# Weight tiles of 16 KiB per partition in place of 8 KiB, and the residual added behind the third expert's gate

## The chip, the cores and the metric

The kernel runs on one core of a Trainium2 chip. The metric is the device time of one execution in microseconds (us). One KiB is 1024 bytes, one MiB 1024 KiB; GB/s are powers of ten.

## The reference

One layer of an encoder over 256 positions of width 2048, in float32. A mixer (attention with forget gates beside a state-space scan, between one input and one output projection) is followed by a mixture of 16 experts, of which each position uses two, and a gated embedding of the layer's own input `p`:

```
h   = layer_norm(ALPHA * h + hybrid_mixer(h), ln1_g, ln1_b)
moe = sum over e of combine[:, e] * ((silu(h @ w_gate[e]) * (h @ w_up[e])) @ w_down[e])
ple = sigmoid(h @ w_ple_gate) * (p @ w_ple)
out = layer_norm(ALPHA * h + moe + ple, ln2_g, ln2_b)
```

`w_gate` and `w_up` are 16 x 2048 x 1024, `w_down` is 16 x 1024 x 2048: 8 MiB each per expert, 384 MiB in all. `w_ple_gate` is 2048 x 2048 (16 MiB).

## The kernel before

**Two halves.** `front` computes the mixer; TensorE is its limit. `back` does the first layer norm, the transposed activations `hT`, the router, the 16 experts, the gated embedding and the last norm. All large weights come through one stream of loads.

**The ring.** `plan_loads` writes a list of loads, in the order in which `back` will use them: `p`, one quarter of column 0 of `w_ple_gate`, and for each expert eight pairs of a gate and an up tile, then eight down tiles. Ahead of the gate of experts 3, 6, 9 and 12 (`PLE_AT`) stand the pieces of one column of 512 of `w_ple_gate` and the piece of `w_ple`. A tile is 128 partitions by 8 KiB, 1 MiB. `Ring` hands out slots: `fill` gives each free slot the next load of the list, and `take` gives the slot of the tile that is about to be used back to the list of free slots. 16 slots go round (pools `ring0` to `ring3`, 4 each), and the pool `bonus` has two that are used once and whose place then becomes the accumulator `acc`. The loads are issued in order on SyncE's queue (SP). A load into a slot waits until TensorE has read the slot's last tile, and with it wait all loads behind it.

**An expert.** `gather` picks the rows of two experts at a time with one-hot matmuls (64 places for each expert; L681). For each expert `gate_up` (L711) makes the two sums `pgu`, `hidden` (L718 to L725) the activated product and its transpose, `down` (L758) the output in the bank `py`, and `give_back` (L735, L739) adds it to `acc` by one-hot matmuls and VectorE. While VectorE and ScalarE work in `hidden`, and between the parts of `give_back`, TensorE's program has matmuls of the next expert's gate. `ple_gate` (L803, L817) comes behind `down` of experts 3, 6, 9 and 12 in the code, and its matmuls L803 are laid between those of the next gate or of the same expert's.

**What stands around the edit.** The first quarter of column 0 (`PLE_FIRST`) is multiplied in the router phase, between the router's matmuls and the first `gather`. `residual` forms ALPHA times the first norm's output: `row_bank` (L882) copies rows of gain and bias to all partitions with matmuls into the bank `py`, which has one buffer, and VectorE multiplies and adds from it into `acc` (L897, L898), in four rounds for four columns of 512. It is issued behind the gate of expert 0. At expert 7 (`OV_AT`) a conditional block for positions that found no place (`overflow`) makes the engines meet.

Of the kernel before, what the change touches and what calls it, by code (L numbers as in the profile page):

```python
# [7 lines left out]
F32 = mybir.dt.float32  # L8
# [16 lines left out]
RING0, RING1, RING2, RING3 = 4, 4, 4, 4  # L25
PLE_AT = (3, 6, 9, 12)
PLE_FIRST = 1
OV_AT = 7

# [9 lines left out]
class Ring:  # L39


    def __init__(self, pool, bufs):
        self.loads, self.n, self.pools, self.spare, self.tiles = [], 0, [], [], {}
        self.once = None
        self.add(pool, bufs)
        self.spare = []
# [26 lines left out]
def plan_loads(nc, ring, i):  # L73

    def rows(src, row0, nrow, col0, ncol):
        return lambda t: nc.sync.dma_start(
            t[:, :nrow // 128 * ncol].rearrange("p (k f) -> p k f", f=ncol),
            src[row0:row0 + nrow, col0:col0 + ncol].rearrange("(k p) f -> p k f", p=128))

    def pairs(src, b):  # L80

        return lambda t: nc.sync.dma_start(t, src[b * 256:(b + 1) * 256, :].rearrange("(p r) f -> p (r f)", r=2))

    def pair_cols(src, g, col0):
        def load(t):
            for b in range(2):
                nc.sync.dma_start(
                    t[:, b * 1024:(b + 1) * 1024].rearrange("p (r f) -> p r f", r=2),
                    src[g * 512 + b * 256:g * 512 + (b + 1) * 256, col0:col0 + 512].rearrange("(p r) f -> p r f", r=2))
        return load  # L90

    def quarter(src, fb0, q):
        def load(t):
            for dh in range(2):
                nc.sync.dma_start(
                    t.rearrange("p (k d f) -> p k d f", d=2, f=256)[:, :, dh, :],
                    src[fb0 * 128:(fb0 + 4) * 128, dh * 1024 + q * 256:dh * 1024 + (q + 1) * 256]
                    .rearrange("(k p) f -> p k f", p=128))
        return load

    L = ring.loads
    L.append(("p", rows(i["p"][0, 0], 0, 256, 0, 256)))
    def ple_gate(c, parts):
        return [(("pg", c, g), pair_cols(i["w_ple_gate"][0], g, c * 512)) for g in parts]

    L += ple_gate(0, range(PLE_FIRST))
    for e in range(NE):
        if e in PLE_AT:
            c = PLE_AT.index(e)
            L += ple_gate(c, range(0 if c else PLE_FIRST, 4))  # L110
            L.append((("ple", c), rows(i["w_ple"][0], 0, 256, c * 512, 512)))
        for k in range(8):
            L.append((("g", e, k), pairs(i["w_gate"][0, e], k)))
            L.append((("u", e, k), pairs(i["w_up"][0, e], k)))
        if e < NE - 1:
            L += [(("d", e, k), rows(i["w_down"][0, e], k * 128, 128, 0, DM)) for k in range(8)]
        else:
            L += [(("d", e, k), quarter(i["w_down"][0, e], 4 * (k % 2), k // 2)) for k in range(8)]


def front(ctx, tc, i, dbg=lambda *a: None):
    nc = tc.nc
    const = ctx.enter_context(tc.tile_pool(name="const", bufs=1))
    ring = Ring(ctx.enter_context(tc.tile_pool(name="ring0", bufs=1)), RING0)
# [36 lines left out]
    for j, n in enumerate(("ln1_g", "ln1_b")):  # L161
        nc.gpsimd.dma_start(lnT[:, j, :].rearrange("p (b r) -> p b r", r=2),
                            i[n][0].rearrange("(b p r) -> p b r", p=128, r=2))
# [3 lines left out]
    for r in range(2):  # L167
        nc.gpsimd.dma_start(fr.wr.rearrange("p (b r) e -> p r b e", r=2)[:, r, :, :NE],
                            i["w_router"].rearrange("(b p r) e -> p r b e", p=128, r=2)[:, r])
# [19 lines left out]
    def load_w(src, row0, nrow, col0, ncol, behind=False):  # L189
        t = ring.tile(0)  # L190
# [287 lines left out]
    ring.add(fr.es_bonus.enter_context(tc.tile_pool(name="bonus", bufs=1, side="right")), 2)  # L478
# [49 lines left out]
    es_mix.close()  # L528
    es_ps.close()
# [3 lines left out]
def back(ctx, tc, i, out, fr, dbg=lambda *a: None):  # L533
# [5 lines left out]
    ring.spare += [0] * RING0  # L539
# [46 lines left out]
    for k2 in range(8):  # L586
        ps = banks[k2].rearrange("p (k t) -> p k t", k=2)
        for r in range(2):
            k = 2 * k2 + r
            for t in range(NT):  # L590
                nc.tensor.transpose(ps[:, r, t * 128:(t + 1) * 128], h[:, t, k2 * 256 + r:(k2 + 1) * 256:2], ident)
# [19 lines left out]
    for t in range(NT):  # L611
        router_mm = nc.tensor.matmul(pr[:, t, :], r4[:, t * 128:(t + 1) * 128], sel4, start=True, stop=True)
# [54 lines left out]
    def gather(e):  # L667
# [7 lines left out]
        for k4 in range(4):  # L675
            ps = mt_psum([128, 4, 2, CAP])
            ks = range(4 * k4, 4 * k4 + 4)
            for k in ks:
                cols = slice(k // 2 * 256 + k % 2, (k // 2 + 1) * 256, 2)
                for t in range(NT):  # L680
                    nc.tensor.matmul(ps[:, k % 4], h[:, t, cols], oh[:, t, :, 0, :], start=t == 0, stop=t == 1)  # L681
# [21 lines left out]
    def gate_up(e, xg):  # L703
        pgu = [psum.tile([128, 512], F32, name="pgu", tag="gu", bufs=2) for _ in range(2)]
        for k2 in range(8):
            for j in range(2):
                w = v2(ring.take(("gu"[j], e, k2)), FE)
                for r in range(2):
                    k = 2 * k2 + r
# [6 lines left out]
    def hidden(pgu):  # L716
# [5 lines left out]
        for j in range(4):  # L722
            nc.tensor.transpose(ps[:, j, :], hid[:, j * 128:(j + 1) * 128], ident)  # L723
# [4 lines left out]
    def give_back(e, cm, y, cols, n, pss):  # L728


        for t in range(NT):
# [5 lines left out]
            for dh, hs in H2:  # L737
                a = acc[:, t, dh * 1024 + cols:dh * 1024 + cols + n]
                nc.vector.scalar_tensor_tensor(a, ps[dh], cw[:, t, e:e + 1], a, op0=OP.mult, op1=OP.add)  # L739
# [11 lines left out]
    def down(e, hidT, cm):  # L751
        py = psum.tile([128, 2, 512], F32, name="py", tag="y", bufs=1)
        for fb in range(8):
            w = ring.take(("d", e, fb))
            fh, j = divmod(fb, 4)
            for c in range(2):
                for dh, hs in H2:
                    nc.tensor.matmul(py[hs, c, :], hidT[:, j, fh * 64:(fh + 1) * 64],  # L758
                                     w[:, dh * 1024 + c * 512:dh * 1024 + (c + 1) * 512],
                                     start=fb == 0, stop=fb == 7)  # L760
            ring.fill()
# [11 lines left out]
    def down_last(e, hidT, cm):  # L773
        py = psum.tile([128, 2, 512], F32, name="py", tag="y", bufs=1)
        y = y_parts()
        for q in range(4):
            pq = py[:, q // 2, (q % 2) * 256:(q % 2) * 256 + 256]
            for f2 in range(2):
                w = ring.take(("d", e, 2 * q + f2)).rearrange("p (k d f) -> p k d f", d=2, f=256)
                for j in range(4):  # L780
                    for dh, hs in H2:
                        nc.tensor.matmul(pq[hs], hidT[:, j, f2 * 64:(f2 + 1) * 64], w[:, j, dh, :],  # L782
                                         start=f2 + j == 0, stop=f2 + j == 4)
                ring.fill()
# [9 lines left out]
    pgs = {}  # L794

    def ple_sums(c, parts):
        pg = pgs[c] = pgs.get(c) or [pl_psum() for _ in range(NT)]
        for g in parts:
            w = v2(ring.take(("pg", c, g)), 512)
            for r in range(4):  # L800
                k = 4 * g + r
                for t in range(NT):
                    nc.tensor.matmul(pg[t], hT[:, k, t * 128:(t + 1) * 128], w[:, r, :],  # L803
                                     start=k == 0, stop=k == KB - 1)
            ring.fill()

    def ple_gate(c):
        cs = slice(c * 512, (c + 1) * 512)
        ple_sums(c, range(0 if c else PLE_FIRST, 4))
        pg = pgs.pop(c)  # L810
        w = v2(ring.take(("ple", c))[:, :1024], 512)
# [10 lines left out]
    def overflow():  # L822
# [9 lines left out]
        with tc.If(n_over > 0):  # L832
            with tc.For_i(0, NE, 1) as e:
# [6 lines left out]
                for fh in range(2):  # L840
                    pgs = [psum.tile([128, 512], F32, name="pgu", tag="gu", bufs=2) for _ in range(NT)]
                    pus = [pl_psum() for _ in range(NT)]
                    for k in range(KB):
                        for j, (src, pz) in enumerate(((i["w_gate"], pgs), (i["w_up"], pus))):
                            w = wload(ow[j], src, e, k // 2 * 256 + k % 2, fh * 512, 2)
# [24 lines left out]

    with tc.issue_after(router_mm.ins):
        ple_sums(0, range(PLE_FIRST))
# [14 lines left out]
    def residual():  # L887

        fr.es_bonus.close()
        accp = ctx.enter_context(tc.tile_pool(name="accp", bufs=1, side="right"))  # L890
        acc = accp.tile([128, NT, DM], F32, name="acc")
        for c in range(4):
# [6 lines left out]
        return acc  # L899

    for e in range(NE):
# [3 lines left out]
        if e == 0:  # L905
            with tc.issue_after(gated.ins):
                acc = residual()
# [79 lines left out]
```

## Time and profile before

| what | value |
|---|---|
| median of three runs | 1470.08 us (1469.17 to 1472.7) |
| the profiled execution | 1471.18 us, its span 1469.5 us |
| TensorE busy (PE) | 1397.5 us, 95% |
| VectorE, ScalarE, GpSimd busy | 459.3, 296.9, 63.0 us |
| moved by DMA | 499.95 MB, mean 340 GB/s |

The expert part runs from about 448 us to 1450 us of the span; what comes before is the mixer, the first norm and the router. On the page the span is cut into 40 slices, so each figure there stands for 36.7 us. PE is TensorE's matmul side, PEld its weight load, DVE VectorE, ACT ScalarE, POOL GpSimd, SP SyncE. A matmul of the source in fp32 is two instructions in the trace. `pgu`, `py`, `mt`, `pl` are PSUM tiles, `ring` a weight tile.

### The profile page before, as it was taken

The page shows a single profiled execution, that of the slowest core. Times are in us where ns is not written, and L with a number is a line of the kernel's source. Part 1 is how long each engine was busy: PE and PEld are TensorE (multiplying, and loading weights), DVE is VectorE, ACT ScalarE, POOL GpSimd, SP SyncE. Part 2 cuts the span into 40 slices and gives each one's busy share as a digit, 9 for nine tenths or more (in the row PEclk, how much of TensorE's full clock was granted, in tenths as well). Part 3 has the DMA queues.
Part 4 walks back from the last instruction along what each step waited for, and adds up shares of the span by engine and source line. Part 5 has one row for each costly group of instructions (what it writes and reads, how often), then busy time and mean ns, then how long its engine had stood idle before and what let it go on. Part 6 is the DMA issues. An engine that isn't in the chain of part 4 may idle for free. (4 is left out here: it accounts for less than half of the span.)

```text
span 1469.5 us, 15853 instructions
## 1 busy us (share of the span) xinstructions
PE 1397.5 (95%) x6531; PEld 722.8 (49%) x6531; DVE 459.3 (31%) x777; ACT 296.9 (20%) x477; POOL 63.0 (4%) x80
## 2 busy tenths in 40 slices
PE   7999999999989999999999999799999999999993
PEld 5877888787884443334324323433343342344332
DVE  4486784646552331202022002112020220202116
ACT  4465554444340010001001000100010010011000
POOL 3000101201000000000000000000000000000002
PEclk9999999999999999999999999999999999999997
DMA  8645456457955799999999999999999999999994
GB/s 268 202 163 182 158 175 227 158 182 278 349 229 231 310 410 420 411 420 419 420 420 409 419 420 420 365 421 408 421 390 420 420 407 420 420 420 419 420 394 160
DMA packets 116720, 499.95 MB, mean 340 GB/s; under 512 B 12692, under 2 KB 25436, under 8 KB 68260
## 3 DMA queue, kind: packets, MB, share of 16 engines
q1 hardware_dynamic: 115200, 495.42, 85.3%
q0 software_dynamic: 1408, 3.43, 0.9%
q8 instruction: 53, 0.87, 0.2%
q14 instruction: 23, 0.19, 0.0%
q10 hardware_dynamic: 36, 0.05, 0.0%
HBM read 496.70 MB, written 2.16 MB: 339 GB/s over the span
## 5 line engine op out<-in xcount | busy, mean ns | idle before, releaser
L711 PE MATMUL pgu<-ring,xg 128*64 128x512 f32 x2048 | 476.8, 598 | 4.4 <-DMA ring<-in_w_gate 2.6
L711 PEld LDWEIGHTS pgu<-ring,xg 128*64 128x64 f32 x2048 | 138.9, 136 | 294.9 <-issue 277.9
L758 PE MATMUL py<-ring,hidT 128*64 128x512 f32 x960 | 209.3, 594 | 4.8 <-ACT hidT L725 4.8
L205 DVE TENSOR_TENSOR wl<-ring,wh 128x1024 fp32r<-128x1024 f32 x128 | 156.3, 1224 | 139.0 <-ACT wh L204 133.8
L204 ACT ACTIVATE wh<-ring 128x1024 fp32r<-128x1024 f32 x128 | 135.4, 1059 | 171.2 <-PE pj L211 151.9
L719 DVE TENSOR_TENSOR hid<-hid,pgu 128x512 f32<-128x512 f32 x16 | 11.0, 687 | 465.6 <-ACT hid L718 465.6
L209 PE MATMUL pj<-wh,xh 128*128 128x512 f32 x384 | 154.2, 403 | 1.1 <-ACT xh L186 1.0
L210 PE MATMUL pj<-wl,xh 128*128 128x512 f32 x384 | 154.0, 402 | 0.0
L211 PE MATMUL pj<-wh,xl 128*128 128x512 f32 x384 | 153.3, 401 | 0.0
L758 PEld LDWEIGHTS py<-ring,hidT 128*64 128x64 f32 x960 | 67.7, 137 | 136.4 <-issue 127.3
L803 PE MATMUL pl<-ring,hT 128*128 128x512 f32 x256 | 127.8, 619 | 0.0
L749 DVE TENSOR_TENSOR y<-py,y 128x512 fp32r<-128x512 f32 (+1 forms) x34 | 22.4, 660 | 256.2 <-ACT y L748 256.2
L718 ACT ACTIVATE hid<-pgu 128x512 f32<-128x512 f32 x16 | 9.6, 597 | 431.9 <-PE pgu L711 431.9
L209 PEld LDWEIGHTS pj<-wh,xh 128*128 128x128 f32 x384 | 72.9, 190 | 18.3 <-ACT xh L186 2.2
L211 PEld LDWEIGHTS pj<-wh,xl 128*128 128x128 f32 x384 | 72.8, 190 | 16.5 <-DVE xl L187 0.2
L210 PEld LDWEIGHTS pj<-wl,xh 128*128 128x128 f32 x384 | 72.8, 190 | 16.2
L803 PEld LDWEIGHTS pl<-ring,hT 128*128 128x128 f32 x256 | 43.0, 189 | 73.0 <-issue 71.2
L748 ACT ACTIVATE y<-py 128x512 fp32r<-128x512 f32 (+1 forms) x34 | 19.5, 572 | 253.6 <-PE py L758 207.5
L681 PE MATMUL mt<-oh,h 128*128 128x128 f32 x512 | 63.8, 287 | 6.3 <-PEq L832 6.3
L681 PEld LDWEIGHTS mt<-oh,h 128*128 128x128 f32 x512 | 63.1, 202 | 7.1 <-issue 7.0
L209 PE MATMUL pj<-wh,moh 128*128 128x512 f32 (+1 forms) x160 | 56.7, 354 | 0.0
L210 PE MATMUL pj<-wl,moh 128*128 128x512 f32 (+1 forms) x160 | 56.5, 353 | 0.0
(259 smaller groups left out, 975.2 us busy)
## 6 DMA issues: line engine op xcount, KB each, us to landing
ring<-in_w_gate SPq DMA_DIRECT2D x128, 1024.0 KB, 18.9
ring<-in_w_up SPq DMA_DIRECT2D x128, 1024.0 KB, 19.0
ring<-in_w_down SPq DMA_DIRECT2D x120, 1024.0 KB, 19.9
ring<-in_w_in SPq DMA_DIRECT2D x48, 1024.0 KB, 5.1
ring<-in_w_out SPq DMA_DIRECT2D x16, 1024.0 KB, 5.7
ring<-in_w_ple_gate SPq DMA_DIRECT2D x32, 512.0 KB, 14.0
ring<-in_w_down SPq DMA_DIRECT2D x16, 512.0 KB, 8.8
xq<-in_x SPq DMA_DIRECT2D x8, 256.0 KB, 9.2
```

What stands on the lines that cost most here:

```text
L204: nc.scalar.activation(h, v, AF.Copy)
L205: nc.vector.tensor_tensor(l, v, h.bitcast(F32), op=OP.subtract)
L209: nc.tensor.matmul(ps, ah, bh, start=first, stop=False)
L210: nc.tensor.matmul(ps, ah, bl, start=False, stop=False)
L211: nc.tensor.matmul(ps, al, bh, start=False, stop=last)
L681: nc.tensor.matmul(ps[:, k % 4], h[:, t, cols], oh[:, t, :, 0, :], start=t == 0, stop=t == 1)
L711: mm = nc.tensor.matmul(pgu[j][hs], xg[:, k, e % 2, :], w[:, r, fh * 512:(fh + 1) * 512], start=k == 0, stop=k == KB - 1)
L719: nc.vector.tensor_tensor(hid, hid, pgu[0], op=OP.mult)
L748: nc.scalar.activation(yh, ps, AF.Copy)
L749: nc.vector.tensor_tensor(yl, ps, yh.bitcast(F32), op=OP.subtract)
L758: nc.tensor.matmul(py[hs, c, :], hidT[:, j, fh * 64:(fh + 1) * 64], w[:, dh * 1024 + c * 512:dh * 1024 + (c + 1) * 512], start=fb == 0, st ...
L803: nc.tensor.matmul(pg[t], hT[:, k, t * 128:(t + 1) * 128], w[:, r, :], start=k == 0, stop=k == KB - 1)
```

## The change

Tiles are 16 KiB per partition, 2 MiB. A gate or up tile holds four rows of the weight per partition, so each expert has 4 + 4 of them; a down tile holds two rows, 4 for each expert. A column of `w_ple_gate` comes in three tiles of six row blocks, 12 of the 16 KiB, and the third also carries the `w_ple` piece. There is no first quarter any more: all of column 0 comes at expert 3. The last expert's down weights come in four tiles of eight DMAs of 256 KB each, where before there were eight tiles of two DMAs of 512 KB. `ring0` is used by the front alone, in its old size, and closed before `back`; the other pools have 2, 2, 1 (bonus) and 4 tiles, so 8 slots go round with the same bytes as before. `residual` is issued behind the gate of expert 2; VectorE makes `part` and GpSimd adds it to `acc`; the first `give_back` writes `acc` instead of adding to it. The order of features over partitions goes with the four rows (`feats`).

```diff
-RING0, RING1, RING2, RING3 = 4, 4, 4, 4
+RING0, RING1, RING2, RING3 = 4, 2, 2, 4
+R = 4
 PLE_AT = (3, 6, 9, 12)
-PLE_FIRST = 1
+RES_AT = 2
...
-        return pool.tile([128, 2048], F32, name=f"ring{j}", tag=f"ring{j}", bufs=bufs)
+        return pool.tile([128, 4096], F32, name=f"ring{j}", tag=f"ring{j}", bufs=bufs)
...
-        return lambda t: nc.sync.dma_start(t, src[b * 256:(b + 1) * 256, :].rearrange("(p r) f -> p (r f)", r=2))
+        return lambda t: nc.sync.dma_start(t, src[b * 128 * r:(b + 1) * 128 * r, :].rearrange("(p r) f -> p (r f)", r=r))
...
+    def gate_third(g, c):
...
+            v = t[:, :3072].rearrange("p (k f) -> p k f", f=512)
...
+                nc.sync.dma_start(v[:, k - 6 * g:k - 6 * g + n, :], rows4[:, k % R:k % R + n, :])
...
+            if end == KB:
+                nc.sync.dma_start(v[:, 4:6, :], i["w_ple"][0][:, cs].rearrange("(k p) f -> p k f", p=128))
...
-    L += ple_gate(0, range(PLE_FIRST))
     for e in range(NE):
         if e in PLE_AT:
             c = PLE_AT.index(e)
-            L += ple_gate(c, range(0 if c else PLE_FIRST, 4))
-            L.append((("ple", c), rows(i["w_ple"][0], 0, 256, c * 512, 512)))
-        for k in range(8):
-            L.append((("g", e, k), pairs(i["w_gate"][0, e], k)))
-            L.append((("u", e, k), pairs(i["w_up"][0, e], k)))
+            L += [(("pg", c, g), gate_third(g, c)) for g in range(3)]
+        for k in range(4):
+            L.append((("g", e, k), wide(i["w_gate"][0, e], k, R)))
+            L.append((("u", e, k), wide(i["w_up"][0, e], k, R)))
         if e < NE - 1:
-            L += [(("d", e, k), rows(i["w_down"][0, e], k * 128, 128, 0, DM)) for k in range(8)]
+            L += [(("d", e, k), wide(i["w_down"][0, e], k, 2)) for k in range(4)]
...
-    with tc.issue_after(router_mm.ins):
-        ple_sums(0, range(PLE_FIRST))
...
             for t in range(NT):
-                nc.vector.tensor_tensor(acc[:, t, cs], h[:, t, cs], gain, op=OP.mult)
-                nc.vector.tensor_tensor(acc[:, t, cs], acc[:, t, cs], bias, op=OP.add)
+                part = mp.tile([128, 512], F32, name="part", tag="w2", bufs=2)
+                nc.vector.tensor_tensor(part, h[:, t, cs], gain, op=OP.mult)
+                nc.vector.tensor_tensor(part, part, bias, op=OP.add)
+                nc.gpsimd.tensor_tensor(acc[:, t, cs], acc[:, t, cs], part, op=OP.add)
...
+        if e == RES_AT:
             with tc.issue_after(gated.ins):
-                acc = residual()
+                residual()
```

TensorE's program in the router phase, from the router's matmuls to the first gate tile, before the change (`mt` in the rows is the router's and the gather's sums, `pl` the embedding's gate, `oh` the one-hot rows, `ring_N` a weight tile; counts are of source matmuls):

```order
L607 MATMUL mt<-hT,wr 32x256 x16
L612 MATMUL mt<-sel_3620,r_3639 128x16 x2
L803 MATMUL pl<-ring_2860,hT 128x512 x6
L652 MATMUL mt<-s_3660,tri 128x16
L653 MATMUL mt<-s_3660,ones 128x16
L654 MATMUL mt<-s_3660,tri 128x16
L803 MATMUL pl<-ring_2860,hT 128x512 x2
L681 MATMUL mt<-oh,h 128x128 x32
L711 MATMUL pgu<-ring_2897,xg 64x512 x4
```

And the same place in the changed program:

```order
L618 MATMUL mt<-hT,wr 32x256 x16
L623 MATMUL mt<-sel_3604,r_3623 128x16 x2
L663 MATMUL mt<-s_3644,tri 128x16
L664 MATMUL mt<-s_3644,ones 128x16
L665 MATMUL mt<-s_3644,tri 128x16
L692 MATMUL mt<-oh,h 128x128 x32
L722 MATMUL pgu<-ring_2862,xg 64x512 x8
```

The eight matmuls of the embedding's gate are gone from here, and a weight tile is now read by eight matmuls instead of four.

TensorE's program at the end of expert 0's gate before the change, where the residual's rounds (L882, `lnr` are the rows of gain and bias) stand among `hidden` (L723) and the gate of expert 1 (L711):

```order
L698 MATMUL mt<-ident,oh 128x128 x2
L882 MATMUL py<-lnr,ident 128x128 x3
L723 MATMUL mt<-ident,hid 128x128 x4
L882 MATMUL py<-lnr,ident 128x128 x5
L711 MATMUL pgu<-ring_3816,xg 64x512 x4
L711 MATMUL pgu<-ring_3818,xg 64x512 x3
L882 MATMUL py<-lnr,ident 128x128 x8
L711 MATMUL pgu<-ring_3818,xg 64x512
L711 MATMUL pgu<-ring_3828,xg 64x512 x4
L711 MATMUL pgu<-ring_3830,xg 64x512 x3
L882 MATMUL py<-lnr,ident 128x128 x8
```

TensorE's program at the end of expert 2's gate in the changed kernel (L774 is `down`, L816 the embedding's gate at expert 3):

```order
L722 MATMUL pgu<-ring_4121,xg 64x512 x8
L888 MATMUL py<-lnr,ident 128x128 x4
L734 MATMUL mt<-ident,hid 128x128 x4
L888 MATMUL py<-lnr,ident 128x128 x28
L774 MATMUL py<-ring_4178,hidT 64x512 x8
L774 MATMUL py<-ring_4180,hidT 64x512 x8
L774 MATMUL py<-ring_4198,hidT 64x512 x8
L774 MATMUL py<-ring_4200,hidT 64x512 x8
L816 MATMUL pl<-ring_4218,hT 128x512
```

The 32 matmuls of the residual's four rounds now stand in one piece ahead of `down`, with nothing of the next expert's gate between them.

## Rows read from the trace of the kernel before

**Rows 1.** The page: busy time of the engines, granted clock and DMA rate by slice.

```profile
PE 1397.5 (95%) x6531; PEld 722.8 (49%) x6531; DVE 459.3 (31%) x777; ACT 296.9 (20%) x477; POOL 63.0 (4%) x80
...
PEclk9999999999999999999999999999999999999997
...
GB/s 268 202 163 182 158 175 227 158 182 278 349 229 231 310 410 420 411 420 419 420 420 409 419 420 420 365 421 408 421 390 420 420 407 420 420 420 419 420 394 160
```

**Rows 2.** The page: the chain that ended last, share of the span by line.

```profile
PE pgu L711 9%; DMA ring<-in_w_up 7%; DMA ring<-in_w_down 5%; PE py L758 4%; PE pl L803 4%; DMA ring<-in_w_ple_gate 1%; PE mt L681 1%; DMA ring<-in_w_gate 1%; PE mt L735 1%; PE pl L817 0%; PE py L735 0%; DVE acc L955 0%; PE py L782 0%; DVE acc L956 0%; ACT y L748 0%; PE mt L723 0%
```

**Rows 3.** Pieces of that chain in order of time: start us, us, what.

```profile
1008.97 1.94 PE pgu L711 x8
...
1063.53 0.44 PE mt L723 x4
...
1122.18 0.70 DVE hid L720
...
1124.27 13.98 PE py L758 x64
...
1180.18 13.88 PE py L758 x64
1194.06 1.05 PE pl L803 x2
...
1201.36 8.59 PE pl L803 x20
...
1284.16 16.75 DMA ring<-in_w_up
...
1446.00 1.96 PE py L782 x14
```

**Rows 4.** Windows: us, busy of PE, PEld, DVE, ACT, POOL, PEclk, DMA share, GB/s.

```profile
490.00:505.00 15.00, 15.00 (x89) 8.31 (x90) 6.84 (x11) 0.00 (x0) 0.00 (x0) 1.00 0.50 207
505.00:520.00 15.00, 15.00 (x72) 5.03 (x70) 1.14 (x2) 0.00 (x0) 0.00 (x0) 1.00 0.92 354
520.00:535.00 15.00, 15.00 (x74) 4.92 (x72) 7.22 (x12) 1.19 (x2) 0.60 (x1) 1.00 0.99 405
...
610.00:690.00 80.00, 78.51 (x333) 30.75 (x330) 12.45 (x21) 6.39 (x14) 0.00 (x0) 1.00 1.02 418
795.00:806.00 11.00, 11.00 (x46) 3.44 (x42) 2.37 (x4) 1.19 (x2) 0.00 (x0) 1.00 1.05 390
925.00:940.00 15.00, 14.60 (x88) 11.37 (x90) 2.76 (x4) 3.02 (x8) 0.00 (x0) 0.84 1.01 417
...
1060.00:1090.00 30.00, 29.30 (x162) 14.88 (x160) 6.51 (x11) 4.81 (x11) 0.00 (x0) 1.00 0.94 383
```

**Rows 5.** Timeline of TensorE from the router to the gate of expert 0.

```profile
440.35 5.40 PE L803 MATMUL pl<-ring,hT 128*128 128x512 f32 x12
...
448.30 7.69 PE L681 MATMUL mt<-oh,h 128*128 128x128 f32 x64
...
455.93 27.69 PE L711 MATMUL pgu<-ring,xg 128*64 128x512 f32 x128
```

**Rows 6.** Timeline of TensorE, the residual behind expert 0's gate.

```profile
490.24 2.04 PE L882 MATMUL py<-lnr,ident 16*128 16x128 f32 x16
...
506.82 13.90 PE L758 MATMUL py<-ring,hidT 128*64 128x512 f32 x64
```

**Rows 7.** Timeline of VectorE, one round of the residual (first and last of four).

```profile
492.32 0.69 DVE L897 TENSOR_TENSOR acc<-h,py 128x512 f32<-128x512 f32 x1 [2.83 <-PE py L882]
...
494.36 0.69 DVE L898 TENSOR_TENSOR acc<-acc,py 128x512 f32<-128x512 f32 x1
```

**Rows 8.** Timeline of TensorE at the overflow block of expert 7.

```profile
925.40 9.76 PE L681 MATMUL mt<-oh,h 128*128 128x128 f32 x64 [6.34 <-PEq L832]
```

**Rows 9.** Groups of instructions: GpSimd's adds of 128x512.

```profile
L819 POOL TENSOR_TENSOR acc<-acc,sg 128x512 f32<-128x512 f32 x8 | 10.1, 1268 | 745.3 <-DVE sg L818 745.3
```

**Rows 10.** The page, DMA issues: count, KB each, us from issue to landing.

```profile
ring<-in_w_gate SPq DMA_DIRECT2D x128, 1024.0 KB, 18.9
```

More of the change, by code (lines that the diff above doesn't have):

```diff
@@ L24, with feats @@
 WB = 3
-RING0, RING1, RING2, RING3 = 4, 4, 4, 4
+RING0, RING1, RING2, RING3 = 4, 2, 2, 4
+R = 4
 PLE_AT = (3, 6, 9, 12)
-PLE_FIRST = 1
+RES_AT = 2
 OV_AT = 7
+def feats(k):
+    return slice(k // R * 128 * R + k % R, (k // R + 1) * 128 * R, R)
 def bcast(src, offset, pattern, parts=128):
@@ L123, in front @@
     const = ctx.enter_context(tc.tile_pool(name="const", bufs=1))
-    ring = Ring(ctx.enter_context(tc.tile_pool(name="ring0", bufs=1)), RING0)
+    ring = Ring()
+    fr0 = ExitStack()
+    ring0 = fr0.enter_context(tc.tile_pool(name="ring0", bufs=1))
     dram = ctx.enter_context(tc.tile_pool(name="dram", bufs=1, space=bass.MemoryType.DRAM))
@@ L166, in front @@
     nc.gpsimd.memset(fr.wr, 0.0)
-    for r in range(2):
-        nc.gpsimd.dma_start(fr.wr.rearrange("p (b r) e -> p r b e", r=2)[:, r, :, :NE],
-                            i["w_router"].rearrange("(b p r) e -> p r b e", p=128, r=2)[:, r])
+    for r in range(R):
+        nc.gpsimd.dma_start(fr.wr.rearrange("p (b r) e -> p r b e", r=R)[:, r, :, :NE],
+                            i["w_router"].rearrange("(b p r) e -> p r b e", p=128, r=R)[:, r])
     fr.rb = const.tile([128, NE], F32, name="rb")
@@ L189, in load_w @@
     def load_w(src, row0, nrow, col0, ncol, behind=False):
-        t = ring.tile(0)
+        t = ring0.tile([128, 2048], F32, name="ring0", tag="ring0", bufs=RING0)
         v = t[:, :nrow // 128 * ncol].rearrange("p (k f) -> p k f", f=ncol)
@@ L477, in front @@
     fr.es_bonus = ExitStack()
-    ring.add(fr.es_bonus.enter_context(tc.tile_pool(name="bonus", bufs=1, side="right")), 2)
+    ring.add(fr.es_bonus.enter_context(tc.tile_pool(name="bonus", bufs=1, side="right")), 1)
     ring.once = len(ring.pools) - 1
@@ L528, in front @@
     es_mix.close()
+    fr0.close()
     es_ps.close()
@@ L678, in gather @@
             for k in ks:
-                cols = slice(k // 2 * 256 + k % 2, (k // 2 + 1) * 256, 2)
+                cols = feats(k)
                 for t in range(NT):
@@ L704, in gate_up @@
         pgu = [psum.tile([128, 512], F32, name="pgu", tag="gu", bufs=2) for _ in range(2)]
-        for k2 in range(8):
+        for b in range(4):
             for j in range(2):
-                w = v2(ring.take(("gu"[j], e, k2)), FE)
-                for r in range(2):
-                    k = 2 * k2 + r
+                w = v2(ring.take(("gu"[j], e, b)), FE)
+                for r in range(R):
+                    k = R * b + r
                     for fh, hs in H2:
@@ L752, in down @@
         py = psum.tile([128, 2, 512], F32, name="py", tag="y", bufs=1)
[L753 to L760, printed above, removed]
+        for b in range(4):
+            w = v2(ring.take(("d", e, b)), DM)
+            for r in range(2):
+                fb = 2 * b + r
+                fh, j = divmod(fb, 4)
+                for c in range(2):
+                    for dh, hs in H2:
+                        nc.tensor.matmul(py[hs, c, :], hidT[:, j, fh * 64:(fh + 1) * 64],
+                                         w[:, r, dh * 1024 + c * 512:dh * 1024 + (c + 1) * 512],
+                                         start=fb == 0, stop=fb == 7)
             ring.fill()
@@ L777, in down_last @@
             pq = py[:, q // 2, (q % 2) * 256:(q % 2) * 256 + 256]
[L778 to L784, printed above, removed]
+            w = ring.take(("d", e, q)).rearrange("p (k d f) -> p k d f", d=2, f=256)
+            for fb in range(8):
+                fh, j = divmod(fb, 4)
+                for dh, hs in H2:
+                    nc.tensor.matmul(pq[hs], hidT[:, j, fh * 64:(fh + 1) * 64], w[:, fb, dh, :],
+                                     start=fb == 0, stop=fb == 7)
             split_y(y, pq, q * 256, 256)
@@ L792, in down_last @@
                     nc.vector.bn_stats(st[:, t, c, :], acc[:, t, c * 256:(c + 1) * 256])
[L794 to L805, printed above, removed]
     def ple_gate(c):
         cs = slice(c * 512, (c + 1) * 512)
-        ple_sums(c, range(0 if c else PLE_FIRST, 4))
-        pg = pgs.pop(c)
-        w = v2(ring.take(("ple", c))[:, :1024], 512)
+        pg = [pl_psum() for _ in range(NT)]
+        for g in range(3):
+            w = v2(ring.take(("pg", c, g))[:, :3072], 512)
+            for k in range(6 * g, min(6 * g + 6, KB)):
+                for t in range(NT):
+                    nc.tensor.matmul(pg[t], hT[:, k, t * 128:(t + 1) * 128], w[:, k - 6 * g, :],
+                                     start=k == 0, stop=k == KB - 1)
+            if g < 2:
+                ring.fill()
+        w = w[:, 4:6, :]
         for t in range(NT):
@@ L905, in back @@
         if e == 0:
+            fr.es_bonus.close()
+            acc = ctx.enter_context(tc.tile_pool(name="accp", bufs=1, side="right")).tile([128, NT, DM], F32, name="acc")
+        if e == RES_AT:
             with tc.issue_after(gated.ins):
-                acc = residual()
+                residual()
         if e == OV_AT:
```

57 lines of the change are left out of this document (27 added, 30 removed).

## The prediction

> **What bounds the kernel now.** I read the page from the top. TensorE is busy 95% of the span, but the DMA rate stands at 400 to 420 GB/s in nearly every slice from the fifteenth on [rows 1]: in the expert part two engines are at their limit together, and the reader is to see that a busy share of 95% does not settle which one sets the end. The chain that ended last says so too: its largest entries are the gate's matmuls, 9% of the span, and the loads of up and down tiles, 7% and 5% [rows 2]. In order of time the chain runs over TensorE alone from 1008.97 to 1284.16 and then over loads to the last down tile [rows 3]. Even while the chain names TensorE the loads go on at about 420: the ring lets them run ahead until it is full, and then a load waits for TensorE to read a tile. So I count on the side of the loads: the end of the kernel is the moment at which the stream starts, plus bytes divided by rate, plus every stretch in which a load waits for a slot. 1 MiB at 420 GB/s takes 2.5 us. Where a window shows less than 420, the shortfall is time lost.
>
> Before the change two such stretches matter. The windows from 490 to 535 show 207, 354 and 405 GB/s [rows 4], that is 7.6 + 2.4 + 0.5 = 10.5 us lost ((420 - 207) / 420 x 15, and so on): there the residual's rounds slow the gate of expert 1 and put off `down` of expert 0 to 506.82 [rows 6]. Around the embedding's gate at expert 9 the rate is 383 for 30 us, 2.6 us lost; at expert 3, from 610 to 690, it is 418 and nothing is lost [rows 4].
>
> **The change, part by part.** The sum goes against the profiled execution, 1471.2 us (span 1469.5 and 1.7 around it), which is 1.1 above the median of the three runs.
>
> *Start of the stream, +5.2 (4.2 to 6.3).* The first quarter's matmuls filled TensorE for 5.4 us of the router phase while VectorE chose the experts, and ended just as the gather began [rows 5]. The gather waits for VectorE's rows, so taking them away does not bring it forward by more than some tenths. But TensorE now idles there. Behind its 6.34 us wait at expert 7 the granted clock was 0.84 in the window, and the same gather took 9.76 us [rows 4, 8] against 7.69 here [rows 5]. So the first gate starts 0 to 2.1 us later; I take 1. The first slot comes free when a tile has been read: 128 instructions take 27.69 us [rows 5], 0.216 each; a tile now has 16 and not 8, which is +1.7. And the quarter's own tile, read before the gather, let 1 MiB move while TensorE gathered; that head start is gone, +2.5.
>
> *The stall of experts 0 and 1 goes, -10.5.* With no residual there, the gate of expert 1 frees 2 MiB each 3.5 us, faster than the 5.0 that a load needs, and `down` of expert 0 follows its gate at once. I see no reason for a remainder.
>
> *The residual at expert 2, and a new stall at expert 3, +22.8 (15 to 27).* The order shows all four rounds in one piece ahead of `down`. The bank `py` has one buffer, so a round is in series: 16 instructions on TensorE, 2.04 us [rows 6], VectorE's four steps, 494.36 + 0.69 - 492.32 = 2.73 [rows 7], and about 0.1 between them, 4.9. (GpSimd's two adds, 1.27 each [rows 9], lie beside the next round.) Four rounds and the 0.7 of the transposes take 20.3 us, where from gate to `down` it otherwise takes 2.1 (1122.18 to 1124.27, [rows 3]): TensorE is held 18.2 longer. Before, the gate of expert 1 covered this; that cover is gone by the order.
>
> TensorE's line: gate of expert 0 from 456.9, `down` at 456.9 + 27.7 + 2.1 = 486.7. From `down` of an even expert to the next one's, with a gather, it is 55.9 (1124.27 to 1180.18); without the gather, whose length is 7.5, 48.4. So `down` of expert 1 starts at 542.6, of expert 2 it could at 591.0, does at 609.2 and ends at 623.1. Then come twelve of the embedding's instructions, 5.4; `give_back` and what goes with it, 3.1 (1194.06 to 1201.36 less four pieces of 1.05 [rows 3]); and the first gate tile, 3.5: it is read at 635.1.
>
> The loads' line: they resume at 456.9 + 3.5 = 460.4 with 18 MiB loaded. All eight slots are filled once the list is through three experts (72 MiB), three embedding tiles (4.5) and five gate tiles (10): 68.5 MiB more, 171.2 us, at 631.6. From there each load needs a tile read. Slots are given back in the order of the code, in which the embedding's tiles of expert 3 come behind its `down` tiles: so the next eight loads wait for the eight gate tiles, and the ninth for the first `down` tile. Gate tiles now come each 6.8 us, since the embedding's matmuls lie between them (1008.97 to 1063.53 for eight [rows 3]). The eighth is read at 635.1 + 47.7 = 682.8, and the ninth load starts after 0.4 of transposes, the gather's 7.7 and a down tile's 3.5, at 694.4. Unhindered it would be 631.6 + 8 x 5.0 = 671.6. The stall is 22.8. It was none in this stretch before, when one of the column's four quarters had been done long before and the residual too. The bounds: 15 if the rounds shorten to VectorE's and TensorE's work half overlapped, 27 if the clock falls in them.
>
> *Later embedding columns, +3 (0 to 7.5).* Three tiles that use 12 of 16 KiB leave the ring 1 MiB shorter than the old pieces did; that is 2.5 us for each of three columns at most, and nothing where TensorE is not behind. I take what one showed before, 2.6, and a little.
>
> *Larger pieces, -6 (-11.6 to 0).* At 420 GB/s each of 16 queues' engines takes 312 ns for 8 KiB; in a stretch that moved the embedding's gate, in pieces of 2 KiB, the rate was 390 [rows 4], 84 ns each. That is 38 ns per KiB; 16 KiB then take 616 ns, 425.6 GB/s, 1.3% more. Of the stream, 358 MiB (all but the 18 at the start and the last expert's 8) go in such pieces, 895 us: -11.6. I take half, for where TensorE paces the loads a faster load only waits longer. [...]
>
> *Small ones.* The last load is a quarter tile with half the matmuls behind it: half of 1.96 [rows 3], -1. The clock in the residual's rounds, where TensorE works 2.04 of each 4.9: 0 to 3.4, +1, by the stretch at expert 7 [rows 4, 8].
>
> Sum: 5.2 - 10.5 + 22.8 + 3 - 6 - 1 + 1 = +14.5, so 1485.7 against the profiled execution and 1484.6 against the median: **1485 us**.
>
> **The rivals.** *The residual doesn't hold TensorE (faster).* If `down` of expert 2 started at 591.0, the first gate tile of expert 3 would be read at 616.9, the eighth at 664.6, and the ninth load would start at 676.2: the stall is 4.6, and the clock's 1 goes. The sum becomes -4.7, 1465.4 on the median. This decides as long as TensorE is held under about 5 us. For it speaks that the rounds are short and before cost TensorE itself nothing; against it the order, with no other work between them, and the bank's one buffer.
>
> *The transfers gain more than I take (no change).* Eight loads are in flight at once now, 18.9 us from issue to landing [rows 10], so a fixed cost of each is already covered, which speaks against it. For it speaks that the rate rose with the piece from 2 to 8 KiB. It needs 427.6 GB/s with nothing given back where TensorE paces: 895 x (1 - 420 / 427.6) = 16, the sum is +4.5 and the time 1474.6, just within what can't be told from none. [...]
>
> *No gain by pieces, and all else at its dear end (slower still).* Pieces at nothing, 6 more; the clock 2.4 more; the later columns 4.5 more: +27.4, 1497.
>
> **How the numbers follow.** My forecast 0.72 (its own range 1477 to 1493), the first rival 0.09, the second 0.07, the third 0.12. About 0.3%, 4.4 us, can be told from no change. Faster: most of the first rival, 0.06. Same: the rest of it, the second, 0.1. Slower: 0.84. The range leaves out the first rival and half of the third: 1472 to 1496.
>
> **What would show it.** In the changed profile: no dip of the DMA rate from 490 to 535 and a dip, to some 300 GB/s, from about 630 to 695; behind the gate of expert 2 four rounds on TensorE, each some 4.9 us apart, and idle time between them released by VectorE; `down` of expert 2 some 20 us behind its gate's end; loads resuming some 5 us later than before at the start; a full-rate stretch at 420 to 426. The prediction is wrong if the rounds overlap, if the undisturbed rate moves by more than 2% either way, or if the loads at expert 3 don't wait although TensorE is late: then the ring was deeper, or the slots came back in another order, than I reckoned.

## The result, and the profile after

The changed kernel takes 1560.15 us (median of 4 runs, 1558.52 to 1563.0) against 1471.38 for the kernel before beside it: a ratio of 1.0607, with a 95% interval of 1.0583 to 1.0631. It is slower, as forecast, but by 89 us and not by 14, and far outside the range. The page of the changed kernel, busy time first, then the granted clock and the DMA rate by slice, and the chain's shares by engine and line:

```profile
PE 1463.8 (94%) x6531; PEld 796.1 (51%) x6531; DVE 459.4 (29%) x777; ACT 296.5 (19%) x477; POOL 73.3 (5%) x90
...
PEclk9999999999989998899999999899999999989997
...
GB/s 276 167 190 162 179 214 174 172 219 312 141 215 417 425 421 365 225 340 231 427 428 414 362 354 427 381 418 422 337 312 427 426 415 322 419 427 356 421 383 89
...
PE 32%; DMA 2%; DVE 2%; ACT 0%; issue 0%; POOL 0%; DVEq 0%; POOLq 0%
```

The same number of instructions keeps TensorE busy 66 us longer than in [rows 1], and the chain is now TensorE's: 32% of the span, and 2% of transfers. The loads run at up to 428 GB/s and then wait, slice after slice. Which instructions became longer shows in the groups by line (busy, mean ns of one, then idle time ahead of them):

```profile
L692 PE MATMUL mt<-oh,h 128*128 128x128 f32 x512 | 120.9, 400 | 7.6 <-PEq L841 6.6 <-DVE oh L683 1.0
L692 PEld LDWEIGHTS mt<-oh,h 128*128 128x128 f32 x512 | 120.1, 329 | 7.9 <-issue 7.9
```

This is the gather. The same groups on the page of before:

```profile
L681 PE MATMUL mt<-oh,h 128*128 128x128 f32 x512 | 63.8, 287 | 6.3 <-PEq L832 6.3
L681 PEld LDWEIGHTS mt<-oh,h 128*128 128x128 f32 x512 | 63.1, 202 | 7.1 <-issue 7.0
```

The line took 63.8 us, with 202 ns for a weight load; now it takes 120.9, and a weight load 329 ns. The timeline of TensorE in the changed kernel (start, duration, what, idle time ahead) shows the first of the eight gathers, and the residual behind the gate of expert 2:

```profile
446.49 0.58 PE L663 MATMUL mt<-s,tri 128*128 128x16 f32 x2 [5.33 <-DVE s L657]
...
448.92 15.17 PE L692 MATMUL mt<-oh,h 128*128 128x128 f32 x64 [0.99 <-DVE oh L683]
464.02 27.69 PE L722 MATMUL pgu<-ring,xg 128*64 128x512 f32 x128
...
605.37 1.15 PE L888 MATMUL py<-lnr,ident 16*128 16x128 f32 x8
606.45 0.74 PE L734 MATMUL mt<-ident,hid 128*128 128x128 f32 x4
607.13 1.15 PE L888 MATMUL py<-lnr,ident 16*128 16x128 f32 x8
611.19 3.75 PE L888 MATMUL py<-lnr,ident 16*128 16x128 f32 x16 [2.91 <-DVE part L902]
617.92 3.75 PE L888 MATMUL py<-lnr,ident 16*128 16x128 f32 x16 [2.98 <-DVE part L902]
624.66 3.75 PE L888 MATMUL py<-lnr,ident 16*128 16x128 f32 x16 [2.98 <-DVE part L902]
631.50 16.70 PE L774 MATMUL py<-ring,hidT 128*64 128x512 f32 x64 [3.10 <-DVE part L902]
```

The gather takes 15.17 us where it took 7.69 [rows 5]. The residual's rounds stand as the order said, but 6.7 us apart, not 4.9: the sixteen instructions take 3.75 us, where they took 2.04 [rows 6]. The windows (PE, PEld, DVE, ACT, POOL busy, granted clock, DMA share, GB/s) say why, and show the loads on both sides of it:

```profile
475.00:500.00 25.00, 23.89 (x114) 8.14 (x112) 1.37 (x2) 1.58 (x3) 0.00 (x0) 1.00 1.01 429
500.00:550.00 50.00, 49.21 (x227) 21.74 (x223) 10.76 (x20) 2.98 (x6) 0.60 (x1) 1.00 1.01 426
...
605.00:632.00 27.00, 15.03 (x74) 13.26 (x72) 11.32 (x17) 0.60 (x1) 9.48 (x8) 0.59 0.59 230
632.00:700.00 68.00, 68.00 (x245) 23.26 (x242) 7.62 (x14) 1.73 (x4) 0.59 (x1) 0.96 0.79 309
```

In the rounds the granted clock is 0.59 over the whole window; windows within it, from 611 to 629, show 0.50, behind TensorE's first wait of 2.91 us. `down` of expert 2 still pays for it: 16.70 us, at a clock of 0.84 from 632 to 648, where it takes 13.90 [rows 6]. The dip from 490 to 535 of [rows 4] is gone, and the dip at expert 3 is there, 230 and then 309 GB/s.

### The profile page after: what moved, and what is told of

Same layout as the page of the kernel before. It is cut to its first block, busy times and chain, and to the rows that moved or that the text cites. A ratio compares the mean times of both kernels' runs of the same rounds, so it can differ in the third digit from the quotient of the medians.

```text
span 1560.9 us, 15506 instructions
## 1 busy us (share of the span) xinstructions
PE 1463.8 (94%) x6531; PEld 796.1 (51%) x6531; DVE 459.4 (29%) x777; ACT 296.5 (19%) x477; POOL 73.3 (5%) x90
## 3 DMA queue, kind: packets, MB, share of 16 engines
q0 software_dynamic: 1472, 3.43, 0.8%
## 5 line engine op out<-in xcount | busy, mean ns | idle before, releaser
L722 PEld LDWEIGHTS pgu<-ring,xg 128*64 128x64 f32 x2048 | 144.3, 138 | 296.9 <-issue 292.9
L774 PE MATMUL py<-ring,hidT 128*64 128x512 f32 x960 | 212.3, 600 | 7.9 <-ACT hidT L736 4.8
L774 PEld LDWEIGHTS py<-ring,hidT 128*64 128x64 f32 x960 | 68.7, 138 | 140.6 <-issue 133.6
L692 PE MATMUL mt<-oh,h 128*128 128x128 f32 x512 | 120.9, 400 | 7.6 <-PEq L841 6.6
L692 PEld LDWEIGHTS mt<-oh,h 128*128 128x128 f32 x512 | 120.1, 329 | 7.9 <-issue 7.9
L816 PE MATMUL pl<-ring,hT 128*128 128x512 f32 x256 | 121.5, 609 | 0.0
L816 PEld LDWEIGHTS pl<-ring,hT 128*128 128x128 f32 x256 | 44.9, 189 | 66.6 <-issue 66.1
## 6 DMA issues: line engine op xcount, KB each, us to landing
ring<-in_w_down SPq DMA_DIRECT2D x60, 2048.0 KB, 16.9
```

Source lines behind the costliest of these rows:

```text
L722: mm = nc.tensor.matmul(pgu[j][hs], xg[:, k, e % 2, :], w[:, r, fh * 512:(fh + 1) * 512], start=k == 0, stop=k == KB - 1)
```

## The experiments

**The gather's step.** The matmul of the gather loads a slice of `h` as its weights. With R = 4 the 128 columns of a slice lie four elements apart, 16 bytes; before the change they lay two apart. The rivals to this are the larger pieces that land in the same memory meanwhile, and the clock. Three runs tell them apart: the changed kernel with the old step in the gather alone, the kernel before with the new one, and the changed kernel with a step of its own in each gather.

```diff
-                cols = feats(k)
+                cols = slice(k // 2 * 256 + k % 2, (k // 2 + 1) * 256, 2)
```

> The changed kernel, with the gather alone reading h in steps of 2 elements as before the change (it then gathers other features than the weight rows in the tile: the output is not the reference's; number and shape of all instructions stay). Theory A: the weight load of a matmul whose columns lie 16 bytes apart is what makes the gather 15 us instead of 7.6; the gather falls to 7.5 to 7.7 us and, TensorE being the chain, eight times 7.4 us come off: 1497 to 1510 us. Rival B: the gather is slow because the larger pieces write into the memory that TensorE reads, or because the clock falls; it stays at 14 to 15 us and the time within 10 us of 1560.

```diff
-                cols = slice(k // 2 * 256 + k % 2, (k // 2 + 1) * 256, 2)
+                cols = slice(k // 4 * 512 + k % 4, (k // 4 + 1) * 512, 4)
```

> The kernel before, with the gather alone reading h in steps of 4 elements (again other features than the weight rows: the output is not the reference's). Theory A: each gather takes about 15 us, eight of them add 59 us of TensorE work, and since the loads have up to a ring of slack the time rises by 35 to 60 us, to 1505 to 1530. Rival B: without 16 KiB pieces the gather stays at 7.7 us and the time within 5 us of 1471.

```diff
-                cols = feats(k)
+                s = (1, 2, 3, 4, 6, 8, 12, 16)[e // 2]
+                cols = slice(k % s, k % s + 127 * s + 1, s)
```

> The changed kernel with a different step in each of the eight gathers: 1, 2, 3, 4, 6, 8, 12 and 16 elements (features and weight rows don't belong together: the output is not the reference's). Theory A: the cost goes with how many elements of a row lie within 16 bytes: 7.5 to 7.7 us at 1 and 2, about 15 at 4 and above and no dearer at 16, something between at 3. Rival C: the cost grows with the step itself: 16 would be far above 15 us.

The first took 1507.06 us (ratio to before 1.0241, 1.0215 to 1.0267): 53 us came off, and the undisturbed gathers take 7.70, with the larger pieces still landing. The second took 1519.37 (1.0316, 1.0297 to 1.0335): 47 us more than the kernel before, with 15.1 in each gather, and no tile in it is larger than before. The larger pieces are out as a cause. The third (one execution, 1542.1 us) gives the prices, TensorE's timeline of that run with the steps 1, 2, 3, 4, 6, 8, 12 and 16 in this order:

```profile
448.20 9.22 PE L693 MATMUL mt<-oh,h 128*128 128x128 f32 x64 [0.99 <-DVE oh L683]
535.36 7.70 PE L693 MATMUL mt<-oh,h 128*128 128x128 f32 x64
693.25 11.32 PE L693 MATMUL mt<-oh,h 128*128 128x128 f32 x64
810.78 15.08 PE L693 MATMUL mt<-oh,h 128*128 128x128 f32 x64
964.44 14.51 PE L693 MATMUL mt<-oh,h 128*128 128x128 f32 x64 [6.56 <-PEq L842]
1103.09 15.44 PE L693 MATMUL mt<-oh,h 128*128 128x128 f32 x64
1224.12 17.28 PE L693 MATMUL mt<-oh,h 128*128 128x128 f32 x64
1383.06 14.12 PE L693 MATMUL mt<-oh,h 128*128 128x128 f32 x64
```

A step of 2 costs 7.70, of 3 11.32 and of 4 15.08, twice that of 2; from 4 on it stays at 14 to 17 us, and 16, at 14.12, is no dearer than 4. So from 4 on the cost does not grow with the distance (rival C is out). The steps 2, 3 and 4 came as theory A had them; the spread from 14 to 17 us it does not explain, and what inside the weight load makes the price, no run shows. The first row stands behind TensorE's idle time in the router phase, at a granted clock of 0.81 (window 448 to 458), so 9.22 is no price of the step 1; the fifth, the step 6, stands behind a wait too, at 0.78 (window 964 to 979). With neighbouring elements and no wait ahead of the gather a later run shows 7.39.

The clock, the other half of rival B, is out as well. The window of the gather at a step of 4 in the run above, and the window of the first gather in the changed kernel, behind its idle time:

```profile
811.00:826.00 15.00, 15.00 (x66) 14.87 (x67) 2.77 (x4) 2.18 (x6) 0.00 (x0) 1.00 1.00 412
```

```profile
449.00:464.00 15.00, 15.00 (x64) 14.90 (x64) 3.31 (x8) 1.50 (x4) 0.00 (x0) 0.87 0.04 17
```

At a step of 4 the gather takes 15.08 us at a granted clock of 1.00 and 15.17 at 0.87, so the clock hardly matters to it. At a step of 2 it does, as the first two gathers of the run with the old step show, the first of them behind the same idle time (clock 0.82 from 449 to 458.4):

```profile
449.04 9.31 PE L692 MATMUL mt<-oh,h 128*128 128x128 f32 x64 [1.00 <-DVE oh L683]
...
536.29 7.70 PE L692 MATMUL mt<-oh,h 128*128 128x128 f32 x64
```

**The change with that cost removed.** To keep 16 KiB pieces and read neighbouring elements, the first norm can write its output with the features in the tiles' order, once, instead of each gather picking them out.

```diff
-    hT = mp.tile([128, KB, 256], F32, name="hT")
...
+    hn = mp.tile([128, NT, DM], F32, name="hn")
+    hf = h.rearrange("p t d -> p (t d)")
+    hT = hf.rearrange("p (k s) -> p k s", s=256)
...
-            v = h[:, t, c * 512:(c + 1) * 512]
+            v = h[:, t, c * 512:(c + 1) * 512].rearrange("p (q r) -> p r q", r=R)
+            o = hn[:, t, c * 512:(c + 1) * 512].rearrange("p (r q) -> p r q", r=R)
...
-                cols = feats(k)
+                cols = slice(k * 128, (k + 1) * 128)
```

> The changed kernel, computing the reference: the first norm writes its output to another tile with the features of a block of 512 put in the order in which the weight tiles have them, so that the transposes and the gather read neighbouring elements; hT takes the place of the old tile. Theory A: the gather takes 7.5 to 7.7 us as at a step of 2, and the time is that of the run with a step of 2, 1507, within 5 us, since the norm's and the residual's strided accesses on VectorE and ScalarE cost little. Rival: strided accesses of the norm or of the residual cost as much again, and the time stays over 1515.

It took 1507.79 us (1.0244, 1.0220 to 1.0267), as expected, and its undisturbed gathers read neighbours:

```profile
537.68 7.39 PE L695 MATMUL mt<-oh,hn 128*128 128x128 f32 x64
```

So without the gather's price the change still costs 35 us.

**The residual.** First two ways to take it off TensorE's way in the changed kernel, then its move alone in the kernel before.

```diff
-RES_AT = 2
+RES_AT = 1
...
-            p2 = psum.tile([128, 2, 512], F32, name="py", tag="y", bufs=1)
-            gain, bias = (row_bank(p2[:, j, :], lna[:, j, :], c) for j in range(2))
+            gain, bias = (row_bank(pl_psum(), lna[:, j, :], c) for j in range(2))
```

> The changed kernel with the residual behind the gate of expert 1 and its rows copied into the two banks pl, which nothing uses there, instead of the one bank py; the order then lays its rounds among the matmuls of the gather. Theory: the 26 us between the gate of expert 2 and its down fall to about 2.5, and as TensorE is the chain the time falls by 18 to 24 us, to 1536 to 1543. Rival: the loads are the limit around expert 3 and the time falls by less than 8 us.

It took 1555.37 (1.0570, 1.0530 to 1.0609), some 5 us less and not 18 to 24; its interval overlaps the changed kernel's, so even the 5 are not clear of noise. The order lays only two matmuls of the gather, 1.30 us, behind each half round, and each next half round waits for VectorE to empty a bank, so TensorE is held again: the gather's first instruction comes at 543.23 and its last ends at 574.14, 31 us for 15. Other banks alone do not help while all four rounds come in one place. The next run gives each round a place of its own, through the same two banks `pl` (on top of the permuted one):

```diff
-RES_AT = 2
+RES_AT = (1, 2, 4, 5)
...
-        if e == RES_AT:
+        if e in RES_AT:
             with tc.issue_after(gated.ins):
-                residual()
+                residual((RES_AT.index(e),))
```

> As the permuted one, with the residual's four rounds spread over experts 1, 2, 4 and 5, one behind each gate, through the two banks pl, so that down waits for none of them. Theory: the 24 us for which TensorE was held at expert 2 go; down of expert 2 comes at 596 to 600; as TensorE is the chain the time falls by 20 to 27 us, to 1480 to 1487 and, if the loads' higher rate (428 in place of 420) then tells, below it, 1465 to 1480. Rival: later columns of the embedding with the coarser ring take the room, and it stays above 1490.

It took 1487.74 (1.0099, 1.0073 to 1.0125), 20 us less, just past the end of the range: that is what the residual's place costs in the changed kernel. `down` of expert 2 starts at 599.5, as expected, but nothing came on top of the hold: the loads' higher rate, which was to bring it under 1480, does not tell. In the kernel before:

```diff
         if e == 0:
+            fr.es_bonus.close()
...
+        if e == 2:
             with tc.issue_after(gated.ins):
-                acc = residual()
+                residual()
```

> The kernel before with the residual alone as in the change: behind the gate of expert 2, into part, added by GpSimd, the first give_back writing acc. Forecast's step: TensorE is held 18 to 26 us ahead of down of expert 2, less the 10.5 us of loads that were lost at experts 0 and 1: 1480 to 1490. Rival: with tiles of 1 MiB the ring has enough ahead, and the time stays within 5 us of 1471.

1484.97 us (1.0089, 1.0064 to 1.0114), 12.5 above before. Windows of this run:

```profile
490.00:505.00 15.00, 15.00 (x72) 4.68 (x70) 2.42 (x4) 1.19 (x2) 0.00 (x0) 1.00 1.01 418
505.00:520.00 15.00, 15.00 (x76) 5.17 (x77) 4.80 (x9) 0.00 (x0) 0.60 (x1) 1.00 1.01 421
520.00:535.00 15.00, 14.59 (x76) 6.34 (x73) 2.16 (x6) 1.58 (x3) 0.00 (x0) 1.00 1.01 420
...
610.00:690.00 80.00, 76.12 (x278) 24.88 (x278) 11.74 (x20) 2.77 (x5) 2.52 (x2) 0.95 0.87 337
```

The loss at experts 0 and 1 is gone, 418 to 421 for the 207, 354 and 405 of [rows 4], and it comes back half as large again at expert 3: 337 for 418 over 80 us, (418 - 337) / 418 x 80 = 15.5 us of loads. Ahead of that TensorE is held from 587.71 to 613.41, 25.7 us in place of 2.1, and the chain of this run names TensorE for 30% of the span and transfers for 5%.

**The first quarter** in the router phase, alone, in the kernel before:

```diff
-PLE_FIRST = 1
+PLE_FIRST = 0
```

> The kernel before without the first quarter of the embedding's column in the router phase (all of it at expert 3). Forecast's step: the stream resumes about 3.5 us later (head start 2.5, gather 0 to 2 later in a lower clock), 1473 to 1477. Rival: nothing, within 2 us.

1476.57 us (1.0032, 1.0021 to 1.0042), 4.1 above before. TensorE waits 5.35 us in the router phase, and the gather behind it takes 9.33 us in a granted clock of 0.82 (window 445 to 460):

```profile
444.39 0.58 PE L652 MATMUL mt<-s,tri 128*128 128x16 f32 x2 [5.35 <-DVE s L646]
...
446.82 9.33 PE L681 MATMUL mt<-oh,h 128*128 128x128 f32 x64 [0.99 <-DVE oh L672]
```

**Piece or tile.** What do the 16 KiB pieces themselves give? The spread version again, with the same slots and the same number and order of instructions on TensorE, but two pieces of 8 KiB per partition in each tile, and without the permuted norm, which it does not need:

```diff
-        return lambda t: nc.sync.dma_start(t, src[b * 128 * r:(b + 1) * 128 * r, :].rearrange("(p r) f -> p (r f)", r=r))
+        return lambda t: nc.sync.dma_start(
+            t.rearrange("p (k f) -> p k f", k=2),
+            src[b * 128 * r:(b + 1) * 128 * r, :].rearrange("(k p r) f -> p k (r f)", k=2, p=128))
...
```

> As the permuted and spread one, with the same 2 MiB tiles and the same order of instructions on TensorE, but each tile as two pieces of 8 KiB per partition, so that the features lie two apart as before the change and no permuting is needed. Theory: the full-rate stretches fall from 427 to 429 GB/s to 419 to 421, and since TensorE is the chain this costs under 6 us: 1484 to 1494. Rival: the rate comes with the 2 MiB of a transfer, not with its pieces: 427 stays. Second rival: the loads are the limit and the time rises by 10 us or more.

It took 1488.88 (1.0109, 1.0092 to 1.0126), 1.1 us above the version with 16 KiB pieces, which no measurement here can tell from nothing. The two differ in more than the pieces: the gather here reads at a step of 2, 7.70 us for 7.39, some 2.5 over eight, so the pieces' own worth is known only to a few us. The window from 475 to 500 of this run and of the one with 16 KiB pieces:

```profile
475.00:500.00 25.00, 23.89 (x116) 8.04 (x113) 1.38 (x2) 1.58 (x3) 0.00 (x0) 1.00 1.01 418
```

```profile
475.00:500.00 25.00, 23.89 (x114) 8.15 (x112) 1.37 (x2) 1.58 (x3) 0.00 (x0) 1.00 1.01 429
```

The rate goes with the piece, 418 GB/s for 429, not with the transfer, 2 MiB in both, and nothing of it shows in the time while TensorE is the chain.

**The kernel before, better.** What the runs say of the residual holds for the kernel before too: there it costs 10.5 us of loads at experts 0 and 1. One round each behind the gates of experts 4, 5, 8 and 10, through the banks `pl` and GpSimd's adds, and nothing else changed, so that place and banks go together here:

```diff
+RES_AT = (4, 5, 8, 10)
...
-            p2 = psum.tile([128, 2, 512], F32, name="py", tag="y", bufs=1)
-            gain, bias = (row_bank(p2[:, j, :], lna[:, j, :], c) for j in range(2))
+            gain, bias = (row_bank(pl_psum(), lna[:, j, :], c) for j in range(2))
...
+        if e in RES_AT:
             with tc.issue_after(gated.ins):
-                acc = residual()
+                residual((RES_AT.index(e),))
```

> The kernel before, its tiles of 1 MiB and its first quarter kept, with only the residual's four rounds spread over experts 4, 5, 8 and 10, one behind each gate, through the two banks pl and added to acc by GpSimd. Theory: the 10.5 us of loads lost at experts 0 and 1 don't come back, down of expert 0 follows its gate at 487, and the time falls by 4 to 10 us, to 1462 to 1468. Rival: the loads lost early are regained by nothing, but TensorE is the limit from expert 9 on anyway, and the time stays within 3 us of 1472.

1462.76 us, ratio 0.9934 (0.9920 to 0.9947): faster than both kernels. `down` of expert 0 starts at 486.35 instead of 506.82 [rows 6], and the window from 490 to 505 moves 418 GB/s instead of 207 [rows 4]. Its chain names TensorE for 33% of the span and transfers for 1%, where the kernel before had 19% and 14%.

## Why the prediction was wrong

**The step that failed is one that was not in the sum.** The section on the change says that "the order of features over partitions goes with the four rows (`feats`)", and the sum prices the gather at its old 7.5 and 7.7 us everywhere: in the step from one `down` to the next, and in the ninth load's wait. The gather's slice went from two elements to four, and with it each of eight gathers from 7.7 to 15.1. The line's busy time rose by 57 us (63.8 to 120.9). Taken back, 53 us come off the changed kernel; put into the kernel before, they cost 47, and the 5.1 us for which TensorE waited for loads there (2.6 + 1.7 + 0.8) are gone with it. The trace of before holds a faint sign of it: the weight loads of the gather there took 202 ns against 189 where the elements are neighbours (L803 in the page of before). None of the prediction's own signs of being wrong points at this: the rounds don't overlap, the rate moved by about 2%, and the loads at expert 3 do wait.

**The rest was forecast at +14.5 and measured at +35** (1507 against 1472). Point by point:

- *Start of the stream, +5.2:* the part that could be measured alone, the missing first quarter, cost 4.1. The forecast had 1 for the later gate and 2.5 for the head start. Right, clock included: the gather behind the wait takes 1.6 us longer (9.33 for 7.69), and the head start is seen, 133 GB/s from 448 to 456 before and 2 GB/s from 447 to 456 in that run. The +1.7 for the larger tile was not taken alone.
- *The stall of experts 0 and 1, -10.5, and the one at expert 3, +22.8:* together +12.3; the move alone measured +12.5 in the kernel before. The places are right, the one dip gone and the other there. The agreement in size is in part luck. By the prediction's own count, of loads, the run in the kernel before lost 15.5 where it had lost 10.5, which would be +5. The chain of that run is TensorE's, and TensorE was held for 23.6 us and not 18.2, since the rounds took up to 6.7 us and not 4.9; how hold and loads make up the 12.5 no run separates. In the changed kernel the residual costs 20 us against a place that hides it.
- *The clock in the rounds, +1 (0 to 3.4):* too small. `down` of expert 2 starts 26.1 us after the first round (605.37 to 631.50) instead of 20.3: 5.8 us, of which 5.1 are the three rounds of 3.75 for 2.04; and `down` itself takes 2.8 longer.
- *Larger pieces, -6:* the rate was right, 425.6 forecast, 426 to 429 measured; no gain can be told from none, 1.1 us. "I count on the side of the loads" was the wrong side for the changed kernel: with the chain on TensorE, a faster load waits longer for its slot.
- *Missing in the sum, a second time:* the order of `give_back`. With tiles of 1 MiB, matmuls of the next gate lie between its parts from the first on; with tiles of 2 MiB the order has, at nine of the fifteen experts in the spread version, five of its matmuls first, and the fifth waits until VectorE has emptied a bank. One such place in the spread version with 16 KiB pieces (L749 is `give_back`, L725 the gate), and one in the kernel before with its residual spread (L736, L712):

```profile
698.22 0.50 PE L749 MATMUL mt<-y,cm 64*128 64x512 f32 x2 [0.23 <-DVE y L766]
699.66 0.46 PE L749 MATMUL mt<-y,cm 64*128 64x512 f32 x1 [0.93 <-DVE acc L754]
700.05 1.81 PE L725 MATMUL pgu<-ring,xg 128*64 128x512 f32 x2
```

```profile
682.12 1.07 PE L712 MATMUL pgu<-ring,xg 128*64 128x512 f32 x2
683.12 0.51 PE L736 MATMUL mt<-y,cm 64*128 64x512 f32 x2
```

The waits of TensorE from 440 us on, summed by what ended them (total us, times, longest), in the spread version with 16 KiB pieces:

```profile
PE mt L737 <- DVE hid L734: 8.7, 12, 0.8
PE mt L749 <- DVE acc L754: 8.5, 9, 1.0
PE mt L695 <- PEq L844: 6.4, 1, 6.4
PE mt L749 <- ACT y L765: 6.3, 9, 0.8
PE mt L666 <- DVE s L660: 5.3, 1, 5.3
PE py L777 <- ACT hidT L739: 4.1, 6, 0.7
PE mt L749 <- DVE y L766: 2.1, 9, 0.2
...
PE mt L695 <- DVE oh L686: 1.0, 1, 1.0
```

The kernel before has no row for `acc`, `y` on VectorE, `s` or `oh`, and neither has it with its residual spread. These four are 8.5 + 2.1 + 5.3 + 1.0 = 16.9 us. Behind the waits in `give_back` the granted clock falls too, to 0.66 from 699 to 704 us, where the kernel before with its residual spread has 1.00 from 682 to 687. The parts in `give_back`, 10.6, are read from the trace: the version with 8 KiB pieces in tiles of 2 MiB has them too and the kernels with tiles of 1 MiB don't, but no run changed the order alone.

So, with the medians: the gather 53, the residual's place 20, and 15 for all the rest; 53 + 20 + 15 = 88 of the 89 us. The 15 is a difference that hides a gain: it compares a version whose residual is out of the way with a kernel before that still pays 10 for its own. Against the kernel before with its residual spread too, 1462.76, the spread version is 25 us slower. Of these, 4.1 were measured alone (the first quarter) and 10.6 are read from `give_back`; the other 10 are open. The lower clock in `give_back` is probably a part of them, and the later embedding columns, +3 in the sum, were never taken alone.

The rivals: that the residual doesn't hold TensorE is refuted by its rows. That the transfers gain more is refuted in the time, though the rate that it asked for, 427.6, came in the full-rate stretches (426 to 429). "Slower still" named the right side for wrong reasons.

## What to carry to other kernels

The layout that made the transfers' pieces longer here also changed the step with which TensorE reads the gather's weights. Price such a read too: a step of 4 elements of 4 bytes took the gather from 7.70 to 15.08 us. Where two engines stand near their limit together, sum the change on both: here the loads' gain, 418 to 429 GB/s, was worth 1.1 us, which can't be told from nothing, once the change had put the end on TensorE. And work that waits for another engine round by round belongs in as many places as it has rounds; here that made the kernel before 0.7% faster.

## What the runs showed of the hardware

- A gather of 64 instructions of 128x128 in fp32 took 7.39 us with neighbouring columns, 7.70 at a step of 2, 11.32 at 3, 15.08 at 4, and 14.12 to 17.28 beyond; 12 was dearer than 16, 17.28 for 14.12, which stays unexplained. At a step of 4 it took 15.08 to 15.17 us whether the granted clock was 1.00 or 0.87; at a step of 2 it went from 7.70 at 1.00 to 9.31 at 0.82.
- ScalarE paid for the step too: the norm's 128x512 pass, read four apart and written in order, took 1312 ns (the spread version with 16 KiB pieces) where it took 804 in the kernel before; on VectorE 739 and 541.
- The transfer rate rose from 418 to 429 GB/s with pieces of 16 KiB in place of 8, at the same 2 MiB of a transfer (windows from 475 to 500).
- While TensorE ran 16 short instructions and then waited about 3 us for VectorE, four times over, the granted clock fell to 0.50 behind the first wait (0.59 over the 27 us of all four), and the instructions went from 2.04 to 3.75 us.
